# Intake of x in a hybrid encoder step: rows fetched one group ahead and before the first weights, the transposed x stored a step later, sample rows doubled into full tiles

## Chip, core and metric

The kernel runs on one core of one Trainium2 chip. The metric is the device time of one execution in microseconds (us); three runs of the kernel before are given by their median. Engines are named as in the profile: PE is TensorE (matmuls; PEld are its weight loads), DVE is VectorE, ACT is ScalarE, POOL is GpSimd, SP is the sync engine, whose queue issues every DMA of this kernel. A kT or group g below is a set of KG = 4 feature tiles of 128 features each; D = 4096 features make NG = 8 groups.

## The reference, cut to what matters

One layer over 256 prompt tokens and 64 sample tokens, all in float32:

```python
h = rmsnorm(x, norm_pre)                    # x: 320 tokens x 4096
proj = h @ w_in                             # 4096 x 14368
q, k, v, g_sb, xbc, z_ssd, dt_raw = split(proj)
o_sb  = rmsnorm(stick_breaking(q, k, v) * silu(g_sb))
o_ssd = rmsnorm(ssd(silu(conv(xbc)), dt_raw) * silu(z_ssd))
m = concat(o_sb, o_ssd) @ w_out             # 4096 x 4096
x = x + rmsnorm(m)
x = x + rmsnorm(sigmoid(x @ w_ple_gate) * (p @ w_ple_proj))
```

New keys, values, convolution rows and states are returned too. Only the way in which x reaches the first product is touched by the change.

## The kernel before, in words

All 320 tokens are the moving columns of every product. Weights come in blocks of 512 rows by 256 columns (512 KB): `weights` (L152) issues the load of a block (L155), ACT casts it to a 12-bit first part `whi` (L158), DVE takes the rest `wlo` (L159). Four `raw` blocks and three pairs `whi`, `wlo` have room. `three` (L162 to L165) multiplies: whi by xhi, whi by xlo, wlo by xhi, each 128 rows by 320 columns, so a block needs 24 matmuls.

`project` (L188) walks over the eight groups of rows. The first call (L316) computes three column blocks at a time, q, k and v of the first two heads, and during it x is taken in: `load_h(g)` (L267) loads the rows of x for group g (two tiles of 128 prompt tokens and one of 64 sample tokens by 512 features, L275), and for each of the four feature tiles transposes the three pieces on PE with an identity matrix (L283, L284, L285: a trio), copies the result from PSUM into `xr` (ACT L287 for odd tiles, DVE L289 for even ones), and splits it into `ahi` (ACT L290) and `alo` (DVE L291). It then stores `xr` to DRAM (L293; read again late in the kernel as the residual), and ACT sums squares of the rows (L296). `project` calls `load_h(g + 1)` during pass g, behind its first column block. The split x stays in SBUF, so all later projections find it there.

Room is bounded by tags: seven tiles of rows of x (`big`), four of `xr` (`group`), and PSUM: four banks of tag `acc`, all held by q and k, and four of tag `aux`, two of them held by v; the other two are left to the transposes.

The order on each engine is not the order of the program text: a planner places each instruction when it reckons that operands and room are there, and takes the earlier one in the text first. `start` and `tick` (L171, L174) keep work behind a projection in generators, which each pass moves one step further. Among the loads that are far behind in the text but need no shared room are the two of `dsk` (L478, in `steps`): every second element of `d_skip`, 16 a row, spread to 64 rows each.

Of the kernel before, what the change touches and what calls it, by code (L numbers as in the profile page):

```python
# [16 lines left out]
P = 128  # L17
D = 4096
TP = 256
TS = 64  # L20
# [10 lines left out]
# Token windows of 128 columns: prompt 0-127, prompt 128-255, and one whose last 64 are the sample.  # L31
WIN = ((0, 128), (128, 256), (192, 320))
# In a row with three convolution columns between prompt and sample.
# [8 lines left out]
def hymba_step(  # L42
# [17 lines left out]
    # what lives in one half of the kernel: the mixers, or the projections behind them  # L60
# [9 lines left out]
    def big(dtype=F32):  # L70
        return pool["wk"].tile([P, 512], dtype, tag="b", name="b", bufs=7)
# [31 lines left out]
    # keeps row > column  # L103
# [5 lines left out]
    # two identities of 32 on top of each other  # L109
# [3 lines left out]
    # Upper bound of the attention scores: huge where a key may be seen, hugely negative elsewhere.  # L113
    # Columns: keys 0-127 x prompt | cache x sample | keys 128-255 x prompt 128-255 | sample keys x sample
    cap = const1.tile([P, 512], F32, name="cap")
    G.memset(cap, -MASKED)
    for c0, n, base in ((0, 128, 0), (320, 128, 0), (448, 64, 64)):
        # keeps column + base - row > 0
        G.affine_select(out=cap[:, c0:c0 + n], in_=cap[:, c0:c0 + n], compare_op=ALU.is_gt,
                        fill=MASKED, base=base, pattern=[[1, n]], channel_multiplier=-1)  # L120
    G.memset(cap[0:64, 448:512], MASKED)
    # 1 where row <= column, by blocks: (0,0) | (0,1) all | (1,1) | sample
# [29 lines left out]
    def weights(src, kg, c0, nk=KG):  # L152
        """nk row tiles of NCOL columns, split exactly into two parts of 12 bits."""
        raw = wp.tile([P, nk, NCOL], F32, tag="raw", name="raw", bufs=4)
        SY.dma_start(raw, src[kg * nk * P:(kg + 1) * nk * P, c0:c0 + NCOL].rearrange("(k p) c -> p k c", p=P))  # L155
        hi = wp.tile([P, nk, NCOL], F32R, tag="whi", name="whi")
        lo = wp.tile([P, nk, NCOL], F32R, tag="wlo", name="wlo")
        S.copy(hi, raw)  # L158
        V.tensor_sub(lo, raw, hi.bitcast(F32))  # L159
        return hi, lo  # L160
# [6 lines left out]
    # Work behind a projection, as generators that pause between their stages; projections take  # L167
    # them one step further with each group of rows, so that the tensor engine finds their operands ready.
    pending = []

    def start(gen, delay=0):  # L171
        pending.append([gen, delay])
# [15 lines left out]
    def project(specs, acts, nk=KG, order=range(NG), ticks=True):  # L188
        """Products of column blocks (matrix, first column, PSUM tag), two feature tiles each, with
        all tokens. acts(kg) gives the kg-th group of rows of the activations, in two parts."""  # L190
        accs = [[ps.tile([P, 512], F32, tag=tag, name="acc", bufs=4)[:, 0:T] for _ in range(2)] for *_, tag in specs]
        ahead = weights(specs[0][0], order[0], specs[0][1], nk)
        for kg in order:
            xhi, xlo = acts(kg)
            for n, ((src, c0, _), acc) in enumerate(zip(specs, accs)):
                if n == 1 and kg != order[-1]:
                    acts(order[order.index(kg) + 1])
                whi, wlo = ahead or weights(src, kg, c0, nk)
                ahead = None
                for f in range(2):  # L200
                    for j in range(nk):
                        fs = slice(f * P, (f + 1) * P)
                        three(acc[f], whi[:, j, fs], wlo[:, j, fs], xhi[:, j, :], xlo[:, j, :],
                              kg == order[0] and j == 0, kg == order[-1] and j == nk - 1)
            if ticks:
                tick()
        return accs
# [5 lines left out]
    def rsqrt_mean(out, total, n, shape):  # L213
        """out = (total / n + EPS) ** -0.5, with one step of Newton's method."""
        v, t = stat(shape), stat(shape)
        S.activation(out, total, AF.Ln, scale=1.0 / n, bias=eps)
        V.tensor_scalar(v, total, 1.0 / n, EPS, ALU.mult, ALU.add)
        S.activation(out, out, AF.Exp, scale=-0.5)
        V.tensor_mul(t, out, out)
        V.scalar_tensor_tensor(out=t, in0=t, scalar=-0.5, in1=v, op0=ALU.mult, op1=ALU.mult)  # L220
        V.scalar_tensor_tensor(out=out, in0=t, scalar=1.5, in1=out, op0=ALU.add, op1=ALU.mult)

    def factor_of(sqs, n):
        """The norm's factor of each token, on all partitions, from partial sums of squares."""
        r = stat()
        pt = aux()
        for i, sq in enumerate(sqs):
            PE.matmul(pt[:, 0:T], ones, sq, start=i == 0, stop=i == len(sqs) - 1)
        rsqrt_mean(r, pt[:, 0:T], n, (P, T))
        return r  # L230
# [7 lines left out]
    class Squares:  # L238
        """Sum over `count` feature tiles of squares; the last one stays apart."""
# [3 lines left out]
        def add(self, make):  # L243
            """make(tile, soon) squares the next feature tile."""
# [20 lines left out]
    h_groups = []  # L265

    def load_h(g):  # L267
        if g < len(h_groups):
            return h_groups[g]
        cs = slice(g * KG * P, (g + 1) * KG * P)  # L270
        xs = []
        for w in range(3):
            n = 64 if w == 2 else P
            x = big()
            SY.dma_start(x[0:n, :], x_sample[0][:, cs] if w == 2 else x_prompt[0][w * P:(w + 1) * P, cs])  # L275
            xs.append(x)
        xr = group()
        ahi, alo = act_group()
        for j in range(KG):
# [5 lines left out]
            PE.transpose(pt[:, 256:320], xs[2][0:TS, js], ident[0:TS, 0:TS])  # L285
# [7 lines left out]
        SY.dma_start(xt_dram[:, g * KG:(g + 1) * KG, :], xr)  # L293
# [21 lines left out]

    qkv0 = project([(w_in[0], 0, "acc"), (w_in[0], OFF_K, "acc"), (w_in[0], OFF_V, "aux")], load_h)  # L316
# [8 lines left out]
    def gate_in(g):  # L325
        """-g, bounded below as the exponential's argument is above."""
        e = small()[:, 0:g.shape[-1]]
        V.tensor_scalar_max(e, g, CLAMP)  # L328
        return e

    def gate_out(es, vals, outs):
        """out = val / (1 + exp(-g)) for each e of gate_in(g); the quotient by one step of Newton's method."""
# [3 lines left out]
        for e, r in zip(es, rs):  # L336
            # 1 + e, scaled into the logarithm's range
            S.activation(r, e, AF.Ln, scale=2.0 ** -62, bias=tiny)  # L338
# [16 lines left out]
    def put_u(i, ap_mul):  # L355
        """Unit i (16 of each mixer) of the mixed output before its norm."""
# [10 lines left out]
    def to_rows(t, h, dst_p, dst_s, n):  # L367
        """A head's keys or values, back in rows of tokens."""
# [50 lines left out]
    def stick(h, i, q, k, vn, ck, cv, gss):  # L419
# [15 lines left out]
        # softplus(z), and log sigmoid(z) over z  # L435
# [33 lines left out]
    def steps():  # L469
        """dt of each token and head (tokens on partitions), dt * a, and decays."""  # L470
# [8 lines left out]
        # columns of the weights: their first parts, their second parts, nothing  # L479
# [24 lines left out]
        # softplus(r) = max(r, 0) + log1p(e), e = exp(-|r|); log1p(e) = 2 atanh(e / (2 + e))  # L504
# [33 lines left out]
    def conv(acc, ct, out):  # L538
        """Causal convolution and SiLU of a channel tile; out has 323 columns, the sample's at XS."""
# [74 lines left out]
    def ssd_heads(u, i, xt, made, ys):  # L614
        """Heads 2u and 2u+1: their outputs (transposed) and final states."""
# [15 lines left out]
        for half in range(2):  # L631
# [18 lines left out]
            # sums of dt * a over s < r <= l; the last 64 columns over all r <= l of the sample  # L650
# [176 lines left out]
    def put_pair(fp, gates, es):  # L827
        """Gated embedding of two feature tiles, with the norm's weight."""
# [9 lines left out]
    def to_token_rows(fp, t):  # L838
        """Of each four feature tiles: 512 columns of each half of the prompt's rows, and the sample's rows
        with the first two tiles, then with the last two."""  # L840
# [9 lines left out]
        if half:  # L850
            pt = aux()
            for i in range(2):
                # a transpose writes from the first row on: the last two's, then the first two's over their head
# [8 lines left out]
    # units: a group's rows of half of the prompt, or two groups' rows of the sample  # L862
# [27 lines left out]
    def some_residuals(count):  # L890
        """The first units' residuals, into SBUF ahead of time."""
# [91 lines left out]
```

## Time and profile before

| what | value |
|---|---|
| median of 3 runs | 2769.45 us |
| lowest, highest | 2768.79, 2770.16 us |
| profiled execution, span from first to last instruction | 2768.3 us |
| PE busy | 2741.7 us (99%) |
| DVE, ACT, POOL busy | 1450.8 (52%), 1110.9 (40%), 241.5 us (9%) |
| mean DMA rate over the span | 150 GB/s |
| intake of x: first DMA to the last accumulation of q, k, v | 0.8 to 107 us |

The profiled execution has no time of its own beside its span in what the profile gives; the median of the runs is 1.15 us above the span. Busy PE counts a matmul from its start to its modelled end, so back-to-back matmuls overlap in it: how fast PE goes is read from the distance of their starts.

### The profile page before, as it was taken

To read this page: it belongs to the slowest core of one execution; us is meant where nothing else is said; L and a number is where in the kernel's file an instruction comes from. 1 tells how busy PE (TensorE), PEld (TensorE's weight loads), DVE (VectorE), ACT (ScalarE), POOL (GpSimd) and SP (SyncE) were. 2 spreads that over 40 slices of the span, in tenths; PEclk is the share of its full clock that TensorE was granted. 3 is DMA by queue.
4 is the path that set the end of the run, shared out by engine and by line. 5 is a ranking of instruction groups with operands and counts; after the bars stand their busy time and mean duration, and the time that the engine had idled before them with its cause. 6 is when DMAs were issued, how large, how long until landed. Compare 5 with 4: busy or idle time off the path is not lost.

```text
span 2768.3 us, 45230 instructions
## 1 busy us (share of the span) xinstructions
PE 2741.7 (99%) x18710; PEld 2713.2 (98%) x18710; DVE 1450.8 (52%) x2155; ACT 1110.9 (40%) x1551; POOL 241.5 (9%) x327
## 2 busy tenths in 40 slices
PE   9999999999999999999999999999999999999998
PEld 8999999999999999999999999999999989999997
DVE  4566666666666534435354453653333386454453
ACT  5443334433344333424333343543333354444441
POOL 0000010010000000000000000000101032121110
PEclk9999999999999999999999999999999999999997
DMA  7645454454454554555555455555444464444442
GB/s 236 194 120 145 132 149 138 127 164 127 143 148 134 149 153 143 151 149 146 152 143 157 140 150 161 168 162 159 148 150 152 137 191 147 150 144 151 149 142 84
DMA packets 419183, 414.13 MB, mean 150 GB/s; under 512 B 21792, under 2 KB 410784, under 8 KB 418976
## 3 DMA queue, kind: packets, MB, share of 16 engines
q1 hardware_dynamic: 418976, 411.24, 50.2%
q8 instruction: 146, 2.39, 0.3%
q14 instruction: 61, 0.50, 0.0%
HBM read 390.64 MB, written 20.55 MB: 149 GB/s over the span
## 4 chain that ended last, share of the span: by engine, by line
PE 96%; issue 1%; POOL 1%; DMA 1%; DVE 0%; ACT 0%; SPq 0%; DVEq 0%; POOLq 0%; ACTq 0%
PE acc L163 30%; PE acc L165 29%; PE acc L164 29%; POOL ug L817 1%; PE px L876 1%; DMA raw<-in_w_in_dram 1%; PE aux L665 1%; PE aux L372 0%; PE aux L492 0%; PE aux L557 0%; PE aux L847 0%; PE aux L453 0%; PE aux L666 0%; PE aux L426 0%; PE aux L651 0%
## 5 line engine op out<-in xcount | busy, mean ns | idle before, releaser
L163 PE MATMUL acc<-ahi,whi 128*128 128x320 f32 x5632 | 1757.6, 312 | 0.0
L165 PE MATMUL acc<-ahi,wlo 128*128 128x320 f32 x5632 | 1741.6, 309 | 3.6 <-DVE wlo L159 3.6
L164 PE MATMUL acc<-alo,whi 128*128 128x320 f32 x5632 | 1742.2, 309 | 1.3 <-DVE alo L819 1.2
L159 DVE TENSOR_TENSOR wlo<-raw,whi 128x1024 fp32r<-128x1024 f32 (+1 forms) x720 | 888.9, 1236 | 1119.6 <-ACT whi L158 1109.6
L158 ACT CAST whi<-raw 128x1024 fp32r<-128x1024 f32 (+1 forms) x720 | 747.1, 1038 | 1369.3 <-PE acc L164 1328.0
L165 PEld LDWEIGHTS acc<-ahi,wlo 128*128 128x128 f32 x5632 | 1058.5, 188 | 5.4 <-DVE wlo L159 5.4
L164 PEld LDWEIGHTS acc<-alo,whi 128*128 128x128 f32 x5632 | 1059.7, 188 | 2.5 <-DVE alo L819 2.3
L163 PEld LDWEIGHTS acc<-ahi,whi 128*128 128x128 f32 x5632 | 1059.3, 188 | 2.5
L252 POOL TENSOR_TENSOR stat<-stat,w 128x320 f32<-128x320 f32 x88 | 117.5, 1335 | 596.8 <-ACT w L779 404.6
L236 POOL TENSOR_TENSOR w<-ug 128x320 f32<-128x320 f32 x26 | 31.1, 1197 | 947.2 <-DVE ug L457 687.5
L335 ACT ACTIVATE w<-w 128x320 f32<-128x320 f32 (+1 forms) x96 | 45.1, 470 | 101.6 <-DVE w L328 101.5
L342 DVE SCALAR_TENSOR_TENSOR w<-w 128x320 f32<-128x320 f32 (+1 forms) x96 | 51.3, 541 | 16.3 <-ACT w L340 16.3
L236 POOL TENSOR_TENSOR w<-w 128x320 f32<-128x320 f32 x29 | 31.1, 1071 | 296.4 <-DVE w L346 296.4
L550 DVE SCALAR_TENSOR_TENSOR w<-w,vec 128x323 f32<-128x323 f32 x96 | 53.1, 553 | 2.1
L338 ACT ACTIVATE w<-w,tiny 128x320 f32<-128x320 f32 (+1 forms) x96 | 52.3, 560 | 2.9
L340 ACT ACTIVATE w<-w,shift 128x320 f32<-128x320 f32 (+1 forms) x96 | 52.2, 559 | 1.4
L344 DVE SCALAR_TENSOR_TENSOR w<-w 128x320 f32<-128x320 f32 (+1 forms) x96 | 49.6, 529 | 1.2
L545 POOL COPY ctail<-w 128x3 f32<-128x3 f32 x32 | 6.1, 190 | 328.3 <-DVE w L543 328.3
L328 DVE TENSOR_SCALAR w<-acc 128x320 f32<-128x320 f32 x32 | 15.6, 488 | 24.8 <-PE acc L165 24.7
L817 POOL TENSOR_TENSOR ug<-ug,two 128x320 f32<-128x320 f32 x16 | 23.7, 1486 | 43.2 <-DVE ug L816 43.2
L818 ACT CAST ahi<-ug 128x320 fp32r<-128x320 f32 x32 | 14.4, 461 | 25.8 <-POOL ug L817 22.4
L636 DVE TENSOR_SCALAR b<-le,dtah 128x256 fp32r<-128x256 f32 (+2 forms) x96 | 24.7, 292 | 0.0
(270 smaller groups left out, 1476.7 us busy)
## 6 DMA issues: line engine op xcount, KB each, us to landing
raw<-in_w_in_dram SPq DMA_DIRECT2D x448, 512.0 KB, 3.7
raw<-in_w_out_dram SPq DMA_DIRECT2D x128, 512.0 KB, 3.6
raw<-in_w_ple_gate_dram SPq DMA_DIRECT2D x128, 512.0 KB, 3.6
xt_dram<-ug SPq DMA_DIRECT2D x8, 640.0 KB, 6.2
two<-xt_dram SPq DMA_DIRECT2D x16, 320.0 KB, 3.3
b<-in_x_prompt_dram SPq DMA_DIRECT2D x16, 256.0 KB, 4.7
out_dram<-nat SPq DMA_DIRECT2D x32, 128.0 KB, 1.8
raw<-in_w_ple_proj_dram SPq DMA_DIRECT2D x16, 256.0 KB, 2.7
```

Source lines behind the costliest of these rows:

```text
L158: S.copy(hi, raw)
L159: V.tensor_sub(lo, raw, hi.bitcast(F32))
L163: PE.matmul(out, whi, xhi, start=start, stop=False)
L164: PE.matmul(out, whi, xlo, start=False, stop=False)
L165: PE.matmul(out, wlo, xhi, start=False, stop=stop)
L236: G.tensor_mul(sq, t, t)
L252: G.tensor_add(self.sum, self.sum, sq)
L338: S.activation(r, e, AF.Ln, scale=2.0 ** -62, bias=tiny)
L340: S.activation(r, r, AF.Exp, scale=-1.0, bias=shift)
L342: V.scalar_tensor_tensor(out=e, in0=e, scalar=1.0, in1=r, op0=ALU.add, op1=ALU.mult)
L550: V.scalar_tensor_tensor(out=c, in0=ext[:, j:j + XE], scalar=vec3[:, j * 32 + ct:j * 32 + ct + 1], in1=c, op0=ALU.mult, op1=ALU.add)
L817: (G if j % 2 else V).tensor_add(m, m, xt[:, j % 2, :])
```

## The change

Before the first projection the rows of group 0 are fetched (`fetch_x(0)`), ahead of the first weights in the text. `load_h(g)` takes rows already fetched, and behind its transposes fetches those of group g + 1. The sample's 64 rows are read twice by one DMA into the two halves of a tile of 128 rows, and the third transpose of each trio is a full 128 by 128 one that writes columns 256 to 383 of the bank; the copies still read 320 columns. The store of `xr` becomes a generator that runs one `tick` later. The squares read 64 rows of the sample as before. The rest of the diff removes comments and docstrings (left out here).

```diff
-    h_groups = []
+    h_groups, x_rows = [], []
+
+    def fetch_x(g):
+        cs = slice(g * KG * P, (g + 1) * KG * P)
+        xs = [big() for _ in range(3)]
+        for w in range(2):
+            SY.dma_start(xs[w], x_prompt[0][w * P:(w + 1) * P, cs])
+        SY.dma_start(xs[2], x_sample[0][:, cs].unsqueeze(0).broadcast_to([2, TS, KG * P]))
+        x_rows.append(xs)
+
+    def store_xt(g, xr):
+        SY.dma_start(xt_dram[:, g * KG:(g + 1) * KG, :], xr)
+        yield 1
 
     def load_h(g):
         if g < len(h_groups):
             return h_groups[g]
-        cs = slice(g * KG * P, (g + 1) * KG * P)
-        xs = []
-        for w in range(3):
-            n = 64 if w == 2 else P
-            x = big()
-            SY.dma_start(x[0:n, :], x_sample[0][:, cs] if w == 2 else x_prompt[0][w * P:(w + 1) * P, cs])
-            xs.append(x)
+        xs = x_rows[g]
         xr = group()
...
             PE.transpose(pt[:, 128:256], xs[1][:, js], ident)
-            PE.transpose(pt[:, 256:320], xs[2][0:TS, js], ident[0:TS, 0:TS])
+            PE.transpose(pt[:, 256:384], xs[2][:, js], ident)
...
-        SY.dma_start(xt_dram[:, g * KG:(g + 1) * KG, :], xr)
+        if g < NG - 1:
+            fetch_x(g + 1)
+        start(store_xt(g, xr), 1)
...
+    fetch_x(0)
     qkv0 = project([(w_in[0], 0, "acc"), (w_in[0], OFF_K, "acc"), (w_in[0], OFF_V, "aux")], load_h)
```

## Rows read from the trace of the kernel before

**Rows 1.** The page: span, and each engine's busy time, share, instructions.

```profile
span 2768.3 us, 45230 instructions
PE 2741.7 (99%) x18710; PEld 2713.2 (98%) x18710; DVE 1450.8 (52%) x2155; ACT 1110.9 (40%) x1551; POOL 241.5 (9%) x327
```

**Rows 2.** Waits of PE, whole run: total us, times, longest.

```profile
PE aux L283 <- ACT ug L287: 2.0, 1, 2.0
```

**Rows 3.** Chain that ended last, group 2's second pair of trios: start, us, what.

```profile
30.84 0.11 PE aux L283
30.95 0.11 PE aux L284
31.06 0.20 PE aux L285
31.26 0.26 PE aux L283
31.52 0.11 PE aux L284
31.63 0.20 PE aux L285
31.84 0.34 PE acc L163
32.18 0.15 PE acc L164
```

**Rows 4.** Full 128 by 128 transposes elsewhere (keys, L372): chain.

```profile
127.13 0.66 PE aux L372 x6
```

**Rows 5.** The same six transposes' loads: lines view, busy us, mean ns.

```profile
L372 PEld LDWEIGHTS aux<-ident,w 128*128 128x128 f32 x6 | 0.7, 139 | 0.0
```

**Rows 6.** ACT and PE timeline around group 2's trios: start, us, what.

```profile
29.05 0.27 PE L283 MATMUL aux<-ident,b 128*128 128x128 f32 x1
29.10 1.04 ACT L158 CAST whi<-raw 128x1024 fp32r<-128x1024 f32 x1 [2.47 <-PE acc L164]
...
30.24 0.43 ACT L287 COPY ug<-aux 128x320 f32<-128x320 f32 x1
```

**Rows 7.** Chain of the start: start, us, what.

```profile
2.74 5.11 DMA b<-in_x_sample_dram
...
8.66 0.21 PE aux L284
...
11.00 0.56 PE acc L163
```

**Rows 8.** Engines in two stretches of the start; last column GB/s.

```profile
3.00:6.00 3.00, 0.05 (x1) 0.06 (x1) 0.00 (x0) 0.95 (x1) 1.28 (x10) 1.00 1.03 353
6.00:8.00 2.00, 1.00 (x3) 0.41 (x3) 1.69 (x5) 0.10 (x1) 0.00 (x0) 1.00 1.01 276
```

**Rows 9.** SP's queue: start, us of issuing, what.

```profile
12.93 1.40 SPq L275 DMA_DIRECT2D b<-in_x_prompt_dram  x2
...
55.71 0.66 SPq L478 DMA_DIRECT2D dsk<-in_d_skip_dram  x1
...
59.12 5.57 SPq L275 DMA_DIRECT2D b<-in_x_prompt_dram  x1
...
68.47 0.63 SPq L478 DMA_DIRECT2D dsk<-in_d_skip_dram  x1
```

**Rows 10.** DMA issues in 55 to 66 us: KB each, median us to landing.

```profile
raw<-in_w_in_dram SPq DMA_DIRECT2D x1, 512.0 KB, 12.8
```

**Rows 11.** DMA issues on the page, whole run.

```profile
raw<-in_w_in_dram SPq DMA_DIRECT2D x448, 512.0 KB, 3.7
```

**Rows 12.** Chain behind the second `dsk` load.

```profile
69.19 14.34 DMA raw<-in_w_in_dram
```

**Rows 13.** The stretch after the wait; before DMA share and GB/s stands PEclk.

```profile
86.20:89.40 3.20, 3.20 (x14) 3.20 (x13) 2.15 (x5) 2.76 (x9) 0.32 (x1) 0.50 1.09 336
```

**Rows 14.** ACT, 15 to 101 us, casts of weights: busy, mean, idle before.

```profile
L158 ACT CAST whi<-raw 128x1024 fp32r<-128x1024 f32 x21 | 21.8, 1045 | 33.0 <-PE acc L164 27.7 <-DMA raw<-in_w_in_dram 5.2
```

## Prediction

> **What bounds the kernel now.** I read the page first. PE is busy for 99% of the span of 2768.3 us [rows 1], and as the chain of work that ended last runs through PE nearly all the way, a microsecond that PE doesn't need in the intake of x comes off the end. Next the waits of PE: in the whole intake only one is in midstream, 2.0 us of a transpose that waits for ACT's copy out of PSUM [rows 2]; the others belong to the start. So the intake is set by PE's own pace, the start, and that wait.
>
> For the pace I read the chain by pieces in group 2. A pair of trios goes 0.11, 0.11, 0.20, 0.26, 0.11, 0.20 us, and the matmul behind it takes 0.34 where the next takes 0.15 [rows 3]. The two long steps stand at every change between a 64-row transpose and a 128-row instruction: into L285, and out of it. Where the kernel transposes full tiles, six take 0.66 us, 0.11 each, with no such steps [rows 4].
>
> For the start I read its chain: the sample rows land 5.11 us after issue at 2.74, thus at 7.85, and the first accumulating matmul starts at 11.00 [rows 7].
>
> For the wait I read SP's queue and the chain behind it. Just behind each of the two `dsk` loads (55.71 and 68.47 us) the queue stalls: the next x load is 5.57 us in issue [rows 9], a block of weights issued near the first takes 12.8 us to land [rows 10], the one behind the second 14.34 [rows 12], against a median of 3.7 [rows 11]. The first stall costs PE nothing. The second keeps ACT in a cast that waits for its block, the copy behind it in ACT's queue comes late, and PE waits its 2.0 us. Then it runs with a granted clock of 0.50, the lower level of 1.2 GHz, from 86.2 to 89.4 us [rows 13], after it had idled.
>
> **The change part by part.**
>
> *Full tiles.* Only the third transpose and its neighbours change. Before, a pair of trios with the matmul behind it costs 0.11 + 0.11 + 0.20 + 0.26 + 0.11 + 0.20 + 0.34 = 1.33 us [rows 3]. After, six steps of 0.11 [rows 4] and a matmul at 0.15 [rows 3] make 0.81. The difference of 0.52 holds for 14 pairs in groups 1 to 7: **-7.3 us**. The bounds are this and nothing (rivals); I take the row of L372, which is the same operation, shape and type at the same clock.
>
> The Trainium skill has a rule against this (TensorE: Matmul & The Clock Gate, Part 3, "What overlaps and what doesn't"): a weight load overlaps a running matmul only when the two sit in different row groups. Full tiles all share their row groups, so by it each transpose would pay its load, and the sum would have no term of -7.3 but about nothing. The trace disagrees: six such loads of 139 ns [rows 5] would need 0.83 us alone, and six transposes with loads took 0.66 [rows 4].
>
> *A wait that comes nearer.* Two PSUM banks are free for transposes, so the fourth trio needs the bank of the second, which ACT's copy frees. In group 2 the first trio starts at 29.05, ACT starts a cast at 29.10 that ends at 30.14, and its copy ends at 30.24 + 0.43 = 30.67 [rows 6]. After the change the fourth trio is ready at 29.05 + 0.66 (a pair) + 0.44 (three matmuls between the pairs) + 0.33 = 30.48, so it waits 0.2 to 0.25 us in each of seven groups if the planner keeps the order. Bounds 0 and 1.75 us; I take **+1.0**.
>
> *x before the first weights.* The sample's third DMA is now third among the large loads, not fourth. In front of its last byte lie 768 KB (two prompt tiles and the doubled sample). From 3.0 us on the queues move 353 GB/s [rows 8], which gives 3.0 + 2.2 = 5.2 us. But before, 1152 KB were needed and 1059 + 510 = 1570 KB had gone by 7.85 [rows 7, 8], as later loads mix in, a factor of 1.36; with it, 1045 KB take 3.0 us and end at 6.0. The sample thus lands 1.9 to 2.6 us earlier. The twelve transposes then need 0.21 each at the start's pace [rows 7], ten of them behind the sample: done at 7.3 to 8.1. The first weights, now behind x, land when 1280 KB have gone: 6.6 us, or with the factor 8.5; the cast of 1.04 [rows 6] ends at 7.7 to 9.5, and if the first `ahi` queues behind it, at 10.0. So accumulation starts between 7.7 and 10.0 instead of 11.00. I take **-2.0**, bounds -3.0 and -1.0. Group 0's saving on transposes is in it.
>
> *Fetched one group ahead.* Nothing: the rows of group 2 were issued at 12.93 us [rows 9] and first transposed at 29.05 [rows 6], so the planner already ran ahead as far as seven tiles allow, and their number stays.
>
> *Doubled sample.* 8 x 128 KB = 1.0 MB more, 3 us of DMA at 353 GB/s [rows 8]. Hidden by the weights' lead: ACT's casts waited 27.7 us for PE to free `whi`, and 5.2 us for weights, all of these in the second stall [rows 14]. If that cover is gone, up to 3 us show.
>
> *Store a step later.* The same eight DMAs, from the same queue. On SP x and weights for the next group no longer stand behind a store that waits for copies; as the weights are ahead, this gives nothing. `xr` is held a pass longer, of four tiles, and a tile is wanted again only three passes later.
>
> *The stall that stays.* The `dsk` loads aren't touched; where the planner puts them I can't know. If they stay, PE meets the stall with less lead: a group gets shorter by 1.04 us of pair time, a third of that for each block, and a block is issued about four casts ahead of its own cast, so the lead shrinks by 1.3 us. The second block then is later by as much: **+1.0**, bounds 0 and +2.5 (the first stall's block too, with some of the clock's loss).
>
> **Sum.** -7.3 + 1.0 - 2.0 + 1.0 = -7.3 us on the span of 2768.3 [rows 1], so 2761.0, and with the 1.15 us between span and median 2762.2. Own range of this case: -7.3 + 0 - 3.0 + 0 gives 2759.1, -7.3 + 1.75 - 1.0 + 2.5 gives 2765.4.
>
> **The rivals.**
>
> *The stall vanishes.* The planner places the `dsk` loads later, or SP, freed of the waiting stores, has its weights issued earlier. For it: the loads stand far behind the intake in the text, and the first stall was hidden already. Against: nothing in the change aims at them, and the demand for weights rises. Then the +1.0 goes, and with it 2.0 us of waiting [rows 2] and the lower clock's cost: 3.2 us at half pace [rows 13], about 1.5. In all -7.3 - 1.0 - 3.5 = -11.8: 2757.7.
>
> *Full tiles bring nothing*, since the long steps come from the end of each bank's group and not from 64 rows. For it: L285 is also the last write of its bank. Against: the six of L372 hold two banks of three and show no step [rows 4]. With PE's third transpose twice as wide (64 columns more, by 320 columns in 0.15 us [rows 3] 0.03 each, 0.9 in all), it is 0 - 2.0 + 0.9: 2768.3, no change.
>
> *The stall is laid bare.* The planner puts both `dsk` loads into the first 40 us, before four blocks of lead stand. Place: SP's queue. Price: the landings of 12.8 and 14.34 against 3.7 [rows 10 to 12] are late by 9.1 and 10.6, 19.7, less the 2.0 already paid, and one more stretch at the lower clock, 1.5: +19.2. With -7.3 + 1.0 - 2.0 that is +10.9: 2780. It turns the sign once 8.3 us of it show, and is slower by over 0.2% from 13.8. For it: the order is the planner's. Against: before they were placed late, and x's DMAs now crowd the early queue.
>
> **Chances.** My sum 0.52, the stall vanishes 0.27, nothing from full tiles 0.11, laid bare 0.10. A time of the likeliest case is forecast: 2762. The range reaches from below the vanishing stall (its 2757.7 less 1.0 for the start and 1.0 for the bank's wait: 2755.7) to the case of no gain: 2756 to 2768, which leaves out the bare stall and half of the no-gain case. 0.2% of the time, about what a measurement here can tell from no change, is 5.5 us: faster means below 2763.9. My sum's range ends at 2765.4, so of its 0.52 some 0.43 is faster and 0.09 the same; with 0.27 faster is 0.70, the same 0.09 + 0.11 + 0.02 (half-bare stalls) = 0.22, slower 0.08.
>
> **What would show it.** Right: in the chain, steps of 0.11 at L285's successor and a matmul of 0.15 behind each pair; the first accumulation starts by 10 us; the intake ends some 7 us earlier. The wait at the bank would be idle time of PE before a transpose, released by ACT's copy, 0.2 us a group. The stall's place shows in SP's queue as a long issue behind `dsk`. Wrong: steps of 0.20 that stay, or PE waits for weights of over 5 us in the intake. What lies behind 107 us should move by less than 1 us; a change there would be the planner's doing and outside this sum.

## The result and the profile after

The changed kernel takes 2796.56 us (median of 4 runs, 2795.97 to 2796.70) against 2769.80 us before; the ratio is 1.0094, with a 95% interval of 1.0080 to 1.0109. It is 26.8 us slower; the forecast was 7.3 us faster. One of the ten executions of a kernel below, the one with two loads, took 5406.84 us, in a slower state, and is left out of its median. The page:

```profile
span 2795.0 us, 45233 instructions
PE 2729.0 (98%) x18710; PEld 2705.2 (97%) x18710; DVE 1448.9 (52%) x2155; ACT 1110.1 (40%) x1551; POOL 242.5 (9%) x327
```

As many PE instructions as before [rows 1], 26.7 us more span, and PE is not busier: it waits. The stretch behind the intake is the same, 2660.0 us from 135 us on against 2661.3 from 107 on, so the intake alone grew by 28 us. The waits of PE (total us, times, longest), next to those of before [rows 2]:

```profile
PE aux L292 <- DMA b<-in_x_sample_dram: 15.5, 3, 6.9
PE aux L291 <- DMA b<-in_x_prompt_dram: 7.6, 1, 7.6
PE aux L290 <- DVE ug L296: 5.1, 2, 4.3
...
PE aux L290 <- DVE n_pre L144: 2.3, 1, 2.3
```

All waits in the intake add up to 37.5 us, against 8.7 before. The largest is for the sample rows: 6.9 and 2.8 us in the first two groups, and 5.9 at 107 us, in midstream. The 7.6 for prompt rows and the 4.3 for a copy also lie late, at 101 and 113 us. The stretches of 8 to 12 us, of 86 to 91 us and of 100 to 110 us (us, busy time and instructions of PE, PEld, DVE, ACT, POOL, granted clock, DMA share, GB/s):

```profile
8.00:10.00 2.00, 0.00 (x0) 0.00 (x0) 0.00 (x0) 0.00 (x0) 0.00 (x0) 1.00 0.64 198
10.00:12.00 2.00, 0.00 (x0) 0.00 (x0) 0.00 (x0) 0.00 (x0) 0.00 (x0) 1.00 0.13 50
...
86.00:91.00 5.00, 5.00 (x36) 5.00 (x35) 0.30 (x1) 0.33 (x2) 0.32 (x1) 1.00 0.05 0
...
100.00:110.00 10.00, 2.38 (x8) 1.69 (x8) 1.23 (x1) 1.04 (x1) 0.00 (x0) 0.50 0.82 261
```

In the second row no compute engine works, and the DMA engines are busy at 0.13: two of 16 would be 0.125. They move 50 GB/s, 25 for each. The Trainium skill names what could do this (DMA: Bandwidth & Descriptors, "Why a DMA increments its semaphore by 16 and not by 1"): a copy is spread over as many engines, up to 16, as divide the slowest dimension of both its sides, and a source `[2, 64, 512]`, as the repeated sample is, would have two. The share of 0.13 agrees. The third row is the stall behind `dsk` known from before, 0 GB/s for 5 us. It is not idle time: in this stretch the DMA engines carry

```profile
DMA packets 542, 0.00 MB, mean 0 GB/s; under 512 B 542, under 2 KB 542, under 8 KB 542
```

which can hardly be anything but the two `dsk` loads' own single elements. These are 2 x 64 x 16 = 2048, and at 542 in 5 us they take 19 us (an estimate). In the fourth row PE has run out of work behind that stall, and the granted clock has fallen to 0.50; it is 1.00 again behind 120 us. What else the trace shows: loads land late, here in 0 to 135 us (KB each, median us to landing; the same lines had 5.7, 6.2 and 4.7 in 0 to 107 us before),

```profile
raw<-in_w_in_dram SPq DMA_DIRECT2D x27, 512.0 KB, 10.5
xt_dram<-ug SPq DMA_DIRECT2D x8, 640.0 KB, 12.1
b<-in_x_prompt_dram SPq DMA_DIRECT2D x16, 256.0 KB, 9.6
```

and the two `dsk` loads now go out together, with a block of weights and an x load stuck behind them (SP's queue: start, us of issuing; before, [rows 9]):

```profile
75.74 3.24 SPq L488 DMA_DIRECT2D dsk<-in_d_skip_dram  x2
79.09 2.15 SPq L155 DMA_DIRECT2D raw<-in_w_in_dram  x1
81.36 9.90 SPq L272 DMA_DIRECT2D b<-in_x_prompt_dram  x1
```

So three suspects: the repeating load, the order of DMAs, and the `dsk` loads. The experiments take them apart.

### The profile page after: what moved, and what is told of

Read it like the earlier page. It is cut to its first block, busy times and chain, and to the rows that moved or that the text cites. A ratio compares the mean times of both kernels' runs of the same rounds, so it can differ in the third digit from the quotient of the medians.

```text
span 2795.0 us, 45233 instructions
## 1 busy us (share of the span) xinstructions
PE 2729.0 (98%) x18710; PEld 2705.2 (97%) x18710; DVE 1448.9 (52%) x2155; ACT 1110.1 (40%) x1551; POOL 242.5 (9%) x327
## 4 chain that ended last, share of the span: by engine, by line
PE 93%; DMA 2%; issue 2%; DVE 1%; SPq 1%; POOL 1%; ACT 1%; DVEq 0%; POOLq 0%; ACTq 0%
PE acc L163 29%; PE acc L165 29%; PE acc L164 29%; DMA raw<-in_w_in_dram 1%; POOL ug L827 1%; DMA b<-in_x_sample_dram 1%; PE aux L675 1%; PE px L886 0%; PE aux L382 0%; PE aux L502 0%; DVE wlo L159 0%; PE aux L567 0%; SPq L272 0%; PE aux L857 0%; PE aux L463 0%
## 5 line engine op out<-in xcount | busy, mean ns | idle before, releaser
L292 PE MATMUL aux<-ident,b 128*128 128x128 f32 x32 | 10.2, 319 | 15.5 <-DMA b<-in_x_sample_dram 15.5
```

## The experiments

Medians; each is compared with the kernel before on the same chip, which was at 2769.8 to 2770.6 us.

**Two loads instead of a repeating one.**

```diff
-        SY.dma_start(xs[2], x_sample[0][:, cs].unsqueeze(0).broadcast_to([2, TS, KG * P]))
+        for half in range(2):
+            SY.dma_start(xs[2][half * TS:(half + 1) * TS, :], x_sample[0][:, cs])
```

> The changed kernel, but the doubled sample rows come by two loads of 64 rows each instead of one load that repeats its source. Theory A (the repeating load moves its 256 KB on two of the 16 DMA engines: in the changed kernel the stretch from 10 to 12 us has a DMA share of 0.13 and 50 GB/s, and the same bytes delay all that is queued on those two engines): no stretch at a share of 0.13 is left in the first 25 us, PE waits no more for sample rows in midstream, and the time is about 2762 us, between 2756 and 2768. Theory B (the order: x ahead of the first weights, and stores a step later, starve the weights): it stays near 2796, at least above 2785. Theory C (the doubled bytes as such, 1 MB more): it stays above 2785 too.

Measured 2773.58 us, ratio 1.0014 (1.0004 to 1.0024). Same bytes, same order, 23.0 us less than the changed kernel: theories B and C can't account for the bulk. But it isn't the 2762 of theory A either, it lies outside its range, and something else costs too.

**64 sample rows again, the rest of the change kept** (load and transpose as in the kernel before).

> The changed kernel with the sample as before: 64 rows loaded and 64-row transposes; fetching ahead, before the first weights, and the later store stay. Theory A: near the kernel before less the earlier start, 2766 to 2770 us, since the full tiles' gain is gone and the load on two engines too. Theory B: above 2785. Theory C: 2766 to 2770.

2775.74 us, ratio 1.0021 (1.0011 to 1.0030). Outside all three: the order costs some 5 us here, by itself or by what it does to the `dsk` loads, which again go out together.

**The repeating load alone, in the kernel before.**

```diff
-            SY.dma_start(x[0:n, :], x_sample[0][:, cs] if w == 2 else x_prompt[0][w * P:(w + 1) * P, cs])
+            if w == 2:
+                SY.dma_start(x, x_sample[0][:, cs].unsqueeze(0).broadcast_to([2, TS, KG * P]))
+            else:
+                SY.dma_start(x, x_prompt[0][w * P:(w + 1) * P, cs])
```

> The kernel before with one edit: the sample's load repeats its source into 128 rows; order, store and the 64-row transposes as before. Theory A: the loss of the change comes with this edit alone, 20 to 35 us over the kernel before, about 2795 us, with stretches of a DMA share near 0.13. Theory B: as before, 2770 us, at most 3 us more. Theory C: as theory A, but without stretches at a share of 0.13.

2788.71 us, ratio 1.0067 (1.0052 to 1.0082): 18.1 us from this one line, a little under the bound of 20. The stretch from 22 to 24 us again has a low DMA share, 0.18, at 58 GB/s.

**Full tiles alone, in the kernel before** (two loads of 64 rows and `PE.transpose(pt[:, 256:384], xs[2][:, js], ident)`).

> The kernel before with full 128-row sample tiles alone, filled by two loads of 64 rows; order and store as before. By the step of the prediction on full tiles: 7.3 us less for the pairs of trios, 1.1 less for the first group, up to 1.75 more for a nearer wait at the PSUM bank, so 2761 to 2764 us, with steps of 0.11 in the chain. If the full tiles bring nothing: 2769 to 2771. Theory C: above 2785.

2768.45 us, ratio 0.9993 (0.9983 to 1.0002): 2 us, which is not clear of no change, and not 7. The trace says where they went. Two rows of SP's queue, the chain behind them, and a wait of PE:

```profile
74.58 2.15 SPq L482 DMA_DIRECT2D dsk<-in_d_skip_dram  x2
...
81.01 10.28 SPq L297 DMA_DIRECT2D xt_dram<-ug  x1
```

```profile
77.13 22.53 DMA raw<-in_w_in_dram
```

```profile
PE aux L317 <- DVE w L316: 7.8, 1, 7.8
```

The planner put the two `dsk` loads next to each other here too, and a block of weights took 22.53 us, against 14.34 behind the second load before [rows 12]. The chain runs on from this block to the end of the intake, where PE waits 7.8 us, against 2.0 in group 6 before [rows 2]. To see the other terms, the next four take this stall out.

**d_skip as plain rows**, in four kernels: before, full tiles alone, the changed kernel with two loads, the changed kernel.

```diff
-        dpair = d_skip[0].rearrange("(u h) -> h u", h=2)
-        for half in range(2):
-            SY.dma_start(dsk[half * 64:(half + 1) * 64, :], dpair[half:half + 1, :].broadcast_to([64, 16]))
+        SY.dma_start(dsr, d_skip[0:1, :].broadcast_to([P, SSDH]))
+        for half in range(2):
+            hp = slice(half * 64, (half + 1) * 64)
+            V.tensor_copy(dsk[hp, :], dsr[hp, :].rearrange("p (u h) -> p h u", h=2)[:, half, :])
```

> The kernel before, with d_skip loaded as plain rows of 128 bytes and spread by two DVE copies, instead of two loads that gather single elements. Theory A2 (the stall of SP's queue comes from the element loads, wherever the planner puts them): no long issue behind the load, no wait of PE in group 6, so 3.5 us less than the kernel before, about 2766 us. Rival (the stall is of the queue at that time, not of these loads): 2769 to 2771.

2766.60 us, ratio 0.9985 (0.9976 to 0.9994): 3.9 us less, and the wait of PE in group 6 is gone. It was these loads, not the queue at that time.

> Full sample tiles by two loads in the order of the kernel before, with d_skip as plain rows. Theory A2 with the prediction's term of 7.3 us for 14 pairs and 1.1 for the first group: 8 us, at most 2 less for the nearer wait at the PSUM bank, below the kernel before with plain d_skip, thus 2758 to 2761. If full tiles bring only the 2 us that they showed with the stall in place: 2764.

2758.97 us, ratio 0.9958 (0.9945 to 0.9971): 7.6 us less than before with plain d_skip, of which 1.7 come at the start: accumulation starts at 10.03 us for 11.71. A pair of trios in the chain, with the matmul behind it:

```profile
51.92 0.15 PE aux L287
52.06 0.11 PE aux L288
52.17 0.11 PE aux L289
52.28 0.19 PE aux L287
52.47 0.11 PE aux L288
52.58 0.11 PE aux L289
52.69 0.15 PE acc L163
```

The 0.20 of the third transpose and the 0.34 of the matmul [rows 3] are gone; the 0.26 between the trios is 0.19.

> The changed kernel with two loads of 64 sample rows and d_skip as plain rows: what stays of the change is order (x before the first weights, fetching one group ahead, the store a step later) and full tiles. Theory D (the order costs about 3 us: the first weights land at 8.5 us instead of 5, and DVE's first copies stand behind their split): 2761 to 2765, 3 to 5 us above the full tiles alone. If the order is worth the 2.0 us of the prediction: 2756 to 2759.

2764.97 us, ratio 0.9982 (0.9973 to 0.9991): 6.0 above full tiles alone, so the order costs even with no stall about. Two pieces of its chain:

```profile
3.45 6.54 DMA raw<-in_w_in_dram
10.01 1.05 ACT whi L158
11.09 1.23 DVE wlo L159
12.31 0.41 DVE ug L297
12.75 0.57 ACT ahi L298
13.36 0.90 PE acc L163 x2
...
22.11 1.85 ACT b L306 x6
23.95 0.73 SPq L274
24.74 0.59 SPq L274
25.42 4.68 DMA raw<-in_w_in_dram
30.20 1.05 ACT whi L158
31.28 1.23 DVE wlo L159
32.50 0.41 DVE ug L297
```

First, the first weights land at 10.0 us, DVE splits them before it makes its first copy of x, and accumulation starts at 13.36, later than the 11.00 of before [rows 7]. In the changed kernel, with its slow sample load, it is 17.56. Second, SP's queue holds an x load that waits for the squares to free its tile, and the weights behind it go out only at 25.42; the cast and the copies behind it follow, and PE waits 1.6 us at 33.

> The changed kernel with d_skip as plain rows, the repeating sample load kept. Theory A: the load on two engines costs 18 us or more by itself, so 2780 to 2790. If the loss came of the two stalls together (element loads behind the slow sample load): within 6 us of the kernel with two loads, below 2770.

2782.58 us, ratio 1.0044 (1.0030 to 1.0057): 17.6 above the kernel with two loads, and 14.0 below the changed kernel, whose `dsk` stall costs that much. The two are not free of each other: with two loads the same stall costs 2773.58 - 2764.97 = 8.6.

**How many engines.** In the changed kernel with plain d_skip, the repeated source gets another shape for the same 256 KB. Both kernels leave out rows of the sample, 56 and 32 of its 64, so that their result is not that of the others; all sizes are the same:

```diff
-        SY.dma_start(xs[2], x_sample[0][:, cs].unsqueeze(0).broadcast_to([2, TS, KG * P]))
+        SY.dma_start(xs[2], x_sample[0][0:8, cs].unsqueeze(0).broadcast_to([16, 8, KG * P]))
```

> The changed kernel with plain d_skip, whose sample load repeats eight rows sixteen times instead of 64 rows twice: the same 256 KB into the same tile, other contents (56 of the sample's rows are left out of the result). Theory A (the number of repeats, the slowest dimension of the source, sets how many DMA engines carry the load): no stretch at a DMA share near 0.13, and near the kernel with two loads, 2763 to 2768. If repeating itself is slow: 2780 to 2785, as with two repeats.

> The changed kernel with plain d_skip, whose sample load repeats 32 rows four times: the same 256 KB, other contents (32 of the sample's rows are left out of the result). Theory A (the repeats set the number of engines): a tail at a DMA share near 0.25 instead of 0.13, half as much extra on each of four engines, and a time between the 2762 us of sixteen repeats and the 2783 of two, nearer the former: 2763 to 2770. If only the two-fold repeat is slow for another reason: 2760 to 2763.

2762.08 us, ratio 0.9970 (0.9959 to 0.9981), for sixteen repeats, and 2769.66, ratio 0.9999 (0.9990 to 1.0008), for four (32 rows), where two took 2782.58. A stretch of the kernel with four repeats:

```profile
16.00:17.00 1.00, 1.00 (x4) 0.60 (x5) 0.85 (x2) 1.00 (x4) 0.00 (x0) 1.00 0.26 88
17.00:18.00 1.00, 1.00 (x5) 1.00 (x6) 0.59 (x2) 1.00 (x4) 0.00 (x0) 1.00 0.28 98
```

Share and rate are twice those of two repeats, and with sixteen no stretch of a microsecond from 8 to 25 us is below 0.40. The median landing of a block of weights in the intake is 10.0 us with two, 8.1 with four, 4.5 with sixteen. Repeating a source costs nothing here; being carried by few engines does. The kernels read 64, 32 and 8 different rows, but that can't be what counts: two plain loads read all 64 and cost little too.

**The order, part by part.** Three edits of the kernel with two loads and plain d_skip (2764.97). They ran on another chip than that kernel; the kernel before took 2770.12 us there and 2770.51 here. Each ratio is known to about 0.1%, some 3 us:

```diff
# weights first: fetch_x(0) is called in load_h(0), behind the first weights
-    fetch_x(0)
# store at once
-        start(store_xt(g, xr), 1)
+        SY.dma_start(xt_dram[:, g * KG:(g + 1) * KG, :], xr)
# fetch in group: fetch_x(g) is called at the head of load_h(g) for g > 0
-        if g < NG - 1:
-            fetch_x(g + 1)
```

> Changed order, two sample loads, plain d_skip (2765 us), with one edit: the first weights are issued ahead of x again. Theory D1 (the start: the first weights land at 10 us instead of 5 and DVE's copies stand behind their split): accumulation starts near 10.5 us instead of 13.4, and the time falls by 2 to 3 us, to 2762 to 2763. Theory D2 (x of the group after next stands in SP's queue in front of weights and waits for tiles that ACT's squares free): no more than 1 us better, 2764 to 2766.

2759.26 us, ratio 0.9959 (0.9946 to 0.9971): 5.7 less, more than either theory gave.

```profile
10.05 0.61 PE L163 MATMUL acc<-ahi,whi 128*128 128x320 f32 x1
```

Accumulation starts 3.3 us earlier, and the waits of PE for copies fall from 5.6 us to 2.0.

> Changed order, two sample loads, plain d_skip, with the store of transposed x at its old place. Theory D3 (the later store costs): 2759 to 2762. Theories D1 and D2: 2764 to 2766.

2762.31 us, ratio 0.9971 (0.9959 to 0.9983): 2.7 less, just outside theory D3, and not clear of no change.

> Changed order, two sample loads, plain d_skip, but from group 1 on the rows are fetched where they were, in front of the group's own transposes; group 0 is still fetched before the first weights. Theory D2: the waits of PE for copies at 33, 43 and 56 us vanish and the time falls by 3 to 5 us, to 2760 to 2762. Theory D1: 2764 to 2766.

2760.43 us, ratio 0.9965 (0.9953 to 0.9978): 4.5 less; PE's waits for copies from 30 us on are gone, though accumulation starts at 13.85. So 5.7, 2.7 and 4.5 together are more than the 6.0 that there are to lose, and weights first alone gives back nearly all of it. I take it that the edits cure the same want of lead; no run shows that by itself.

**The old order with the later store alone.** Weights first and fetch in group together.

> Full sample tiles by two loads and plain d_skip; first weights ahead of x, rows fetched in front of their own transposes, only the later store kept of the changed order. If the two costs of the order (start, and x in front of weights in SP's queue) are separate: below each of the kernels with one of them, 2756 to 2758. If the later store costs too: 2759 to 2761, above the 2759 of full tiles with the old order.

2758.06 us, ratio 0.9958 (0.9945 to 0.9972), 0.9 below full tiles with the old order and the store at once: the same within what can be measured. In the old order the later store costs nothing. The two, and weights first at 2759.26, are the fastest kernels here, 11 to 12 us below the kernel before.

## Why the prediction was wrong

The terms, from kernel to kernel with plain d_skip: 2766.6, full tiles -7.6, order +6.0, the load on two engines +17.6, which gives 2782.6; with the `dsk` loads as they are +14.0. Before, those loads cost 3.9, so against the kernel before it is -3.9 - 7.6 + 6.0 + 17.6 + 14.0 = 26.1 us; the other 0.7 of the 26.8 is how far the kernel before differs between the two measurements. That the steps add up is so by construction. Their sizes depend on the order in which they are taken, the `dsk` loads' most of all.

**The step that failed: "Doubled sample".** I priced it as 1.0 MB more at 353 GB/s over all engines, 3 us of DMA, hidden by the weights' lead. It cost 17.6 us, and 18.1 by itself in the kernel before. The rate held for loads spread over 16 engines. Divided over two, 128 KB a load and engine at 25 GB/s is 5 us, and the other loads land late with it: a median of 10.0 us for a block of weights, against 6.1 with two loads. No row of before had such a load, and I asked only how many bytes it moves.

**"The stall that stays", +1.0.** This step failed too. The stall stayed, but the mechanism that I gave for its price, a lead shorter by 1.3 us (1.04 / 3 times four casts is 1.4), was not what happened. It cost 14.0 us for the 3.9 of before, 10.1 more. The planner puts the two loads back to back, in the changed kernel and in all but one of the first four experiments, and in place of two stalls of which one was hidden there is one of twice the length. My rival "laid bare" had a price of that kind (+19.2 for both, where the runs show 8.6 to 14.0) but the wrong place: they came not early but together. In full tiles alone these loads cost 2768.45 - 2758.97 = 9.5 us where before they cost 3.9, which took 5.6 of the 7.6 us.

**"x before the first weights", -2.0.** The sign was wrong. The sum took the first weights' landing at 6.6 to 8.5 and let the copies run beside it. With two loads they landed at 10.0, and the copies stand behind the split on DVE, which I left out: in the trace of before DVE makes `wlo` first too. Weights first again gives 5.7 us, with 3.3 of it at the start.

**"Fetched one group ahead" and "store a step later", nothing each.** Fetching ahead was wrong in the new order: fetched in the group, 4.5 less. For the store it stays open: stored at once, 2.7 less there, and no difference in the old order. The seven tiles allow no more lead, as I said, but the place in the text moves x loads in front of weights in SP's queue, where they wait for a tile. That weights had lead to spare did not hold once x was fetched ahead.

**"Full tiles", -7.3, and the nearer wait, +1.0.** The mechanism was right and the size near, but that 7.6 and 7.3 agree is in part luck: the 7.6 hold 1.7 us of the start, which my sum had under x before the first weights. Groups follow at 11.98 us (trios at 51.92 and 63.90 in the kernel with full tiles) for 12.94 before (29.05 and 41.99), 0.96 for two pairs where I had 1.04, or 6.7 us for seven groups. The wait at the bank came once, 0.2 us; I had 1.0 in all. The Trainium skill's rule on weight loads (TensorE: Matmul & The Clock Gate, Part 3, "What overlaps and what doesn't"), weighed ahead, would have left no gain. The steps of 0.11 us in the pair above, shorter than such a load of 139 ns [rows 5], decide against it for these transposes.

**The bound of the range** was also wrong in kind: 2768 left out every case in which the intake starves, at 0.08 for slower.

## What to carry to other kernels

Ask of a new DMA not only how many bytes it moves but over how many engines: a load that repeats its source twice ran on two and delayed all the others, and two plain loads did the same work. To fetch earlier is not free where one queue issues everything in order: what moves to the front may wait there for its room, with something more urgent behind it. When a good edit shows no gain, look whether it moved an old stall; here plain d_skip had to go in before 7.6 us could be seen.

## What was not expected of the hardware

A pair of loads of 64 x 16 single elements, 4 KB each, held up SP's queue for 12 us behind it (2.15 and 9.90 us of issuing), with 0 GB/s from 86 to 91 us and only 542 small packets carried; 16 KB in rows of 128 bytes showed no stall. And some 25 GB/s for each engine held for two engines (50) and, nearly, for four (88 to 98).
